# Gated linear unit of a hybrid decoder layer taken in halves by position, with a new written order of the work around it

## The chip, the cores and the metric

The kernel runs on one core of one Trainium2 chip. The metric is the device time of one execution in microseconds. The engines are named as in the profile: PE (TensorE matmuls), PEld (its weight loads), DVE (VectorE), ACT (ScalarE), POOL (GpSimd) and SP (SyncE, which issues the DMAs here).

## The reference

One decoder layer on 1024 positions with 1024 channels, in f32. The input projection z = x w_in is cut into S5 input, S5 gate gs, latents of attention, and an attention gate gm. What the change touches is the S5 head group:

```python
z = x @ w_in[i]
xs, gs, cq, ckv, kr, gm = jnp.split(z, IN_SPLIT_POINTS, axis=-1)
# s5_branch: diagonal complex state space over positions, then
y = jax.nn.gelu(y)
y = y * jax.nn.sigmoid(y @ w_glu.astype(f32) + b_glu.astype(f32))
...
ys = s5_branch(xs, ...) * jax.nn.silu(gs)
ym = mla_branch(cq, ckv, kr, cos, sin, ...) * jax.nn.silu(gm)
mix = jnp.concatenate([ys, ym], axis=-1) @ w_out[i]
u = DEEPNORM_ALPHA * x + mix
ple = jax.nn.sigmoid(u @ w_pg[i]) * (p[i] @ w_pp[i])
x = layer_norm(u + ple, ln_g[i], ln_b[i])
```

The attention has 4 heads, causal, with 1024 queries and keys.

## The kernel before, in words

Activations lie with channels on the 128 partitions and positions along the free axis. Every f32 operand of a matmul is split into a rounded high part and the rest (names ending in h and l: wh, wl; yTh, yTl; ysh, ysl): `split` makes the high part with a cast on ACT or DVE and the low part with a subtraction on DVE or POOL. A product is then three matmuls into the same PSUM tile (`mm3`). Matmuls move at most 512 columns, so most things come in two halves of 512, called hf 0 and 1.

The stages, in the order in which the PE goes through them: the products of p (pp), the layer norm and transposes of x (xt), the projections of the S5 input (xs, L743), then the list MAIN: eight half tiles of the attention gate (gm, L763), eight tiles of latents (lat, L787) and eight half tiles of the S5 gate (gs, L753). A projection half tile is 24 matmuls of 512 columns. Each needs its weight loaded (`w_load`, 512 KB from HBM) and split (`w_split`, tiles wh and wl); the latents need four weights split by `wt_split` (wth, wtl). Then comes attention over the 16 items of ATTEND (a head h and a block j of 256 queries): scores, softmax on DVE and ACT, transposes of the probabilities, product with the latent values, and uv_out, which multiplies by the gate gm and writes ymh and yml. Then the output projection (op) for eight channel tiles m and two halves, which reads ysh, ysl of the S5 group and ymh, yml of attention, and last the gate with p (g) and the final layer norm.

The S5 layer works on 8 interleaved phases: position 8n + j is held as phase j, index n, so that a scan has 128 steps. Its four blocks b each have `mats` (three pieces, DVE and PE), `in` (a load), `usplit`, `state` (tiles re, im, rt, hh, hu; the scans on DVE) and `out` (gelu, and a store to d_y). `glu_y(k)` (L1256) loads block k's y, laid out as phase j by index n, and splits it into yTh and yTl. `glu_gs(m)` (L1264) loads the S5 gate back from d_gs. `glu(m, hf)` (L1268) forms one of eight GLU half tiles: 12 matmuls of 512 columns, a sigmoid, a product with y, a product with the gate, and a split into ysh and ysl. A half here is four of the eight phases, so it covers all positions at a stride; the gate is stored in that layout as well (L753), and the split writes through `perm`, at a stride of 8 elements, into the order of positions that the output projection reads.

Other work hangs on the steps: the lists S5, LAT and GLU say at which step (a half tile or latent tile of MAIN, or an item of attention) a piece is written into the program. The order in which engines get instructions is not this written order. The class Plan records all operations with what they read and write, and `issue` (L304) places them one by one: always the operation that can start soonest by its own table of costs, and among those that can start at once the one with the lowest priority number. That number is the place in the written order plus a shift: SHIFT gives one per list (S5 -350, LAT -750, GLU -1250: these operations go ahead of that many written before them), AHEAD adds one per kind of piece (empty before), and in attention S5's shift is S5_LATE. Tiles come from pools with fixed numbers of buffers (40 of 4 KB per partition, 12 of 2 KB, 4 single and 2 double PSUM banks) and are given out in the written order, so this order decides also who gets a buffer first. For operations that may run on either of two engines (a split's high part on ACT or DVE, its low part on DVE or POOL) the planner chooses. All instructions are issued from L437, so the profile shows this one line and they are told apart by their tiles.

Of the kernel before, what the change touches and what calls it, by code (L numbers as in the profile page):

```python
# [25 lines left out]
F32 = mybir.dt.float32  # L26
F32R = mybir.dt.float32r
I32 = mybir.dt.int32
AF = mybir.ActivationFunctionType
# [5 lines left out]
P = 128  # L35
S = 1024
D = 1024
NK = D // P
H = 4
G = 32  # L40
CT = 8
NCH = S // CT
# [10 lines left out]
def _cw_parts(c, bits, n):  # L53
# [11 lines left out]
PI_LO = float(np.nextafter(np.float32(math.pi), np.float32(0)))  # L65

MAIN = [
    ("w_load", 10), ("gm", 0, 0), ("gm", 0, 1), ("w_split", 9), ("w_load", 11), ("gm", 1, 0), ("gm", 1, 1),
    ("w_split", 10), ("wt_load",), ("gm", 2, 0), ("gm", 2, 1), ("w_split", 11), ("gm", 3, 0), ("gm", 3, 1),
    ("wt_split", 0), ("wt_split", 1), ("wt_split", 2), ("wt_split", 3), ("lat", 0), ("lat", 1), ("lat", 2),  # L70
    ("lat", 3), ("w_load", 4), ("lat", 4), ("lat", 5), ("w_load", 5), ("lat", 6), ("lat", 7), ("w_split", 4),
    ("w_load", 6), ("gs", 0, 0), ("gs", 0, 1), ("w_split", 5), ("w_load", 7), ("gs", 1, 0), ("gs", 1, 1),
    ("w_split", 6), ("gs", 2, 0), ("gs", 2, 1), ("w_split", 7), ("gs", 3, 0), ("gs", 3, 1),
]


S5 = [
    (0, "in", 0), (0, "mats", 0), (0, "mats", 0), (0, "mats", 1), (0, "mats", 0), (0, "usplit", 0), (0, "state", 0),
    (2, "mats", 1), (5, "in", 1), (5, "mats", 1), (5, "usplit", 1), (5, "out", 0), (7, "mats", 2), (7, "state", 1),
    (7, "out", 1), (8, "mats", 2), (8, "mats", 2), (9, "phase", 1), (9, "in", 2), (13, "usplit", 2),  # L80
    (14, "state", 2), (14, "mats", 3), (16, "out", 2), (16, "in", 3), (18, "mats", 3), (23, "mats", 3),
    (25, "usplit", 3), (27, "state", 3), (30, "out", 3),
]
LAT = [
    (4, "lat_alloc"), (18, "lat_norm", 0), (19, "lat_transpose", 0), (19, "lat_norm", 1), (19, "lat_transpose", 1),
    (20, "fold"), (20, "q_rope", 0), (23, "q_rope_t", 0), (23, "q_rope", 1), (23, "mask"), (23, "q_nope", 0, 0),
    (24, "q_nope", 0, 1), (24, "q_rope_t", 1), (27, "q_nope", 1, 0), (27, "q_nope", 1, 1), (27, "q_nope", 2, 0),
    (28, "q_nope", 2, 1), (35, "q_nope", 3, 0), (35, "q_nope", 3, 1),
]
GLU = [  # L90
    (31, "glu_y", 0), (31, "glu_w"), (33, "glu_gs", 1), (35, "glu_y", 2), (35, "glu_gs", 2), (36, "glu_y", 1),
    (39, "glu_gs", 0), (39, "glu_gs", 3), (39, "glu_y", 3), (40, "glu", 0, 0), (40, "wo_load", 1),
    (41, "glu", 0, 1), (41, "wo_load", 0), (41, "glu", 1, 0), (42, "glu", 1, 1), (42, "glu", 2, 0),
    (42, "wo_split", 0), (42, "glu", 2, 1), (42, "glu", 3, 0), (42, "glu", 3, 1),
]
GATE = [(t, 0) for t in range(3)] + [(t, 1) for t in range(3)] + [(t, c) for t in range(3, 8) for c in range(2)]
ATTEND = [(h, j) for h in range(H) for j in (0, 3, 1, 2)]
S5_LATE = -400
AHEAD = {}
SHIFT = [(S5, -350), (LAT, -750), (GLU, -1250)]  # L100


class _Engine:
# [337 lines left out]
def trunk(ctx, tc, I, out):  # L441
# [10 lines left out]
    dr = ctx.enter_context(tc.tile_pool(name="dr", bufs=1, space=DRAM))  # L452
# [3 lines left out]
    def nm(s):  # L456
        cnt[0] += 1
        return f"{s}{cnt[0]}"

    def U(name, dt=F32, shape=(P, 1024)):  # L460
        return plan.own(up.tile(list(shape), dt, name=nm(name), tag="u"), "u", NU)

    def Hf(name, dt=F32, shape=(P, 512)):
        return plan.own(hp.tile(list(shape), dt, name=nm(name), tag="h"), "h", NHF)
# [10 lines left out]
    def PB(name, shape=(P, 512), dt=F32):  # L475
        return plan.own(psB.tile(list(shape), dt, name=nm(name), tag="B"), "B", 4)

    def f(ap):
        return ap.bitcast(F32)

    def mul(o, a, b, e=V):
        e.tensor_tensor(out=o, in0=a, in1=b, op=ALU.mult)
# [4 lines left out]
    def sub(o, a, b, e=V):  # L487
        e.tensor_tensor(out=o, in0=a, in1=b, op=ALU.subtract)
# [7 lines left out]
    def act(o, a, fn, scale=1.0, bias=None, accum=None):  # L496
        kw = {}
        if bias is not None:
            kw["bias"] = bias
        if accum is not None:  # L500
            kw["accum_out"] = accum
        A.activation(out=o, in_=a, func=fn, scale=scale, **kw)

    def cpy(e, o, a):
        plan.copy(e._name, o, a)

    def split(hi, lo, src, eh=AV, el=None):
        cpy(eh, hi, src)
        sub(lo, src, f(hi), el or (V if src.space == PSUM else VG))

    def mm(ps, a, b, st, sp_):
        T.matmul(ps, a, b, start=st, stop=sp_)

    def mm3(ps, ah, al, bh, bl, st, sp_):
        mm(ps, ah, bh, st, False)
        mm(ps, ah, bl, False, False)
        mm(ps, al, bh, False, sp_)
# [23 lines left out]
    def pexp(o, x, shape):  # L541
# [25 lines left out]
        out=ident, in_=ident, pattern=[[-1, P]], compare_op=ALU.is_equal, fill=0.0, base=0, channel_multiplier=1  # L567
# [16 lines left out]
    d_y = dr.tile([4, CT, P, NCH], F32, name="d_y")  # L584
    d_k = dr.tile([4, 15, 16, P], F32, name="d_k")
    d_gm = dr.tile([4, P, S], F32, name="d_gm")
    d_gs = dr.tile([4, P, CT, NCH], F32, name="d_gs")
    d_ut = dr.tile([8, P, D], F32, name="d_ut")


# [139 lines left out]
    def proj(m, hf):  # L730
        h, l = wq[m]
        ps = PB("z")
        s = slice(hf * 512, hf * 512 + 512)
        for k in range(NK):
            mm3(ps, h[:, k], l[:, k], xh[k][:, s], xl[k][:, s], k == 0, k == NK - 1)
        return ps

    def perm(ap):
        return ap.rearrange("p (n j) -> p j n", j=CT)
# [11 lines left out]
    gs = {}  # L751

    def gs_tile(m, hf):  # L753
        ps = proj(4 + m, hf)
        if hf == 0:
            gs[m] = U("gs", shape=(P, CT, NCH))
        act(gs[m][:, :, hf * 64 : hf * 64 + 64], perm(ps), AF.Silu)
        if hf == 1:
            SY.dma_start(out=d_gs[m], in_=gs[m])

# [482 lines left out]
    Y = {}  # L1243
    ysT = {}
# [17 lines left out]
        Y[k] = y, h, l  # L1262

    def glu_gs(m):  # L1264
        g = Y["gs", m] = U("gsr", shape=(P, CT, NCH))
        SY.dma_start(out=g, in_=d_gs[m])

    def glu(m, hf):  # L1268
        if hf == 0:
            ysT[m] = U("ysh", F32R), U("ysl", F32R)  # L1270
        ps = PB("glu")
        s = slice(hf * 512, hf * 512 + 512)
        for k in range(4):
            wh, wl = Y["w", k]
            ms = slice(m * P, m * P + P)
            mm3(ps, wh[:, ms], wl[:, ms], Y[k][1][:, s], Y[k][2][:, s], k == 0, k == 3)
        sg = Hf("sg")
        act(sg, ps, AF.Sigmoid, bias=Y["b"][:, m : m + 1])
        mul(sg, sg, Y[m][0][:, s])
        sg = sg.rearrange("p (j n) -> p j n", j=4)  # L1280
        j4 = slice(hf * 4, hf * 4 + 4)
        mul(sg, sg, Y["gs", m][:, j4])
        split(perm(ysT[m][0])[:, j4], perm(ysT[m][1])[:, j4], sg)


    uT = {}
# [182 lines left out]
    mats = [s5_mats(b) for b in range(4)]  # L1469
    for m in range(4):  # L1470
# [13 lines left out]
        "mats": lambda b: next(mats[b], None), "phase": s5_phase, "in": s5_in, "usplit": s5_usplit,  # L1484
        "state": s5_state, "out": s5_out, "lat_alloc": lat_alloc, "lat_norm": lat_norm,
        "lat_transpose": lat_transpose, "fold": fold, "q_rope": q_rope, "q_rope_t": q_rope_t,
        "q_nope": q_nope, "mask": mask_init, "glu_w": glu_w, "glu_y": glu_y, "glu_gs": glu_gs, "glu": glu,
        "wo_load": wo_load, "wo_split": wo_split,
    }

    main = {
        "w_load": w_load, "w_split": w_split, "wt_load": wt_load, "wt_split": wt_split,
        "gm": gm_tile, "lat": lat_tile, "gs": gs_tile,
    }
    steps = [0]

    def after(late=False):
        for stream, shift in SHIFT:
            for at, name, *args in stream:
                if at == steps[0]:  # L1500
                    plan.shift = (S5_LATE if stream is S5 and late else shift) + AHEAD.get(name, 0)
                    work[name](*args)
        plan.shift = 0
        steps[0] += 1

    for name, *args in MAIN:
        main[name](*args)
# [110 lines left out]
```

## Time and profile before

| | |
|---|---|
| median of 3 runs | 610.16 us (607.33 to 611.25) |
| the profiled execution | 605.49 us |
| its span, first to last instruction | 603.8 us |
| mean granted PE clock | 0.986 |
| HBM traffic | 50.47 MB read, 25.66 MB written |

How to read the profile: a stage's row gives, for a stretch of the span, the busy time of each engine with its number of instructions, the granted PE clock as a share of full speed, the busy share of the DMA engines and GB/s. A row of waits names who waited, for whom, total us, times, and the longest. A row of groups gives engine, operation, out<-in, shape and count, then busy time and mean ns of one, then the engine's idle time before them. A timeline row gives start and duration in us, and in brackets the idle time before it and what ended it. In the rows of one tile's instructions the durations are min/median/max in ns, with the first and last start.

### The profile page before, as it was taken

Reading aid. Unit: us, or ns where it says so; the run is one execution under the profiler, and the core shown is the slowest. Engines: PE = TensorE matmul, PEld = TensorE weight load, DVE = VectorE, ACT = ScalarE, POOL = GpSimd, SP = SyncE. Lnnn points to the kernel's source line nnn. Section 1 sums busy time; section 2 is a strip of 40 time slices with the busy share of each in tenths; the row PEclk is TensorE's granted clock in tenths of the full one; section 3 lists DMA queues with packets and bytes.
Section 4 is the critical chain, followed back from the end, with each engine's and each line's share of the span. In section 5 each row is a group of like instructions: output and inputs, shape, how many; then the busy total and the mean of one; then the engine's idle time right before and its main releaser. Section 6 shows DMA issues by size and latency. Waiting matters only on the chain.

```text
span 603.8 us, 8361 instructions
## 1 busy us (share of the span) xinstructions
PE 569.3 (94%) x3000; PEld 484.9 (80%) x3000; DVE 447.7 (74%) x958; ACT 287.2 (48%) x527; POOL 83.1 (14%) x104
## 2 busy tenths in 40 slices
PE   8999989699899999999799999996999999999994
PEld 6777878587698888889699999874888888888884
DVE  6999999999989774677979888686323225567666
ACT  6767245463643853357579667552222135233121
POOL 0100001200201133041432313103000001000000
PEclk9999999989999999999999999997999999999998
DMA  8898233620330511201024224425242426924301
GB/s 314 322 356 283 94 105 108 209 72 37 110 104 1 192 69 41 69 37 36 0 71 141 67 75 146 141 87 219 71 139 71 156 85 241 354 78 167 105 35 71
DMA packets 46233, 76.66 MB, mean 127 GB/s; under 512 B 4384, under 2 KB 27104, under 8 KB 46192
## 3 DMA queue, kind: packets, MB, share of 16 engines
q1 hardware_dynamic: 46192, 76.14, 36.6%
q8 instruction: 23, 0.38, 0.3%
q14 instruction: 18, 0.15, 0.1%
HBM read 50.47 MB, written 25.66 MB: 126 GB/s over the span
## 4 chain that ended last, share of the span: by engine, by line
PE 52%; DVE 8%; ACT 3%; DMA 1%; issue 1%; POOL 1%; DVEq 0%; ACTq 0%; POOLq 0%
PE g L437 14%; PE op L437 14%; PE s L437 6%; PE z L437 5%; PE o L437 3%; PE pt L437 2%; DVE sg L437 2%; PE qn L437 1%; DVE ysl L437 1%; PE ut L437 1%; DMA yT<-d_y 1%; ACT ysh L437 1%; PE qrp L437 1%; PE y L437 1%; DVE rt L437 1%
## 5 line engine op out<-in xcount | busy, mean ns | idle before, releaser
L437 PE MATMUL z<-xh,wl 128*128 128x512 f32 x192 | 75.6, 395 | 6.3 <-DVE wl L437 6.3
L437 PE MATMUL z<-xh,wh 128*128 128x512 f32 x192 | 75.7, 394 | 0.0
L437 PE MATMUL z<-xl,wh 128*128 128x512 f32 x192 | 75.6, 394 | 0.0
L437 PE MATMUL g<-wph,uh 128*128 128x512 f32 (+1 forms) x136 | 51.4, 378 | 0.0
L437 PE MATMUL g<-wph,ul 128*128 128x512 f32 (+1 forms) x136 | 51.2, 377 | 0.0
L437 PE MATMUL g<-wpl,uh 128*128 128x512 f32 (+1 forms) x136 | 51.2, 377 | 0.0
L437 DVE SCALAR_TENSOR_TENSOR xr<-xr,op 128x512 f32<-128x512 f32 x16 | 11.0, 687 | 51.9 <-PE op L437 51.9
L437 PEld LDWEIGHTS z<-xh,wl 128*128 128x128 f32 x192 | 36.2, 188 | 13.9 <-DVE wl L437 7.2
L437 PEld LDWEIGHTS z<-xh,wh 128*128 128x128 f32 x192 | 36.2, 189 | 7.0
L437 PEld LDWEIGHTS z<-xl,wh 128*128 128x128 f32 x192 | 36.1, 188 | 6.7
L437 PE MATMUL op<-ysh,woh 128*128 128x512 f32 x64 | 26.8, 419 | 4.4 <-DVE ysh L437 4.4
L437 PEld LDWEIGHTS g<-wpl,uh 128*128 128x128 f32 x136 | 25.6, 188 | 4.7
L437 PEld LDWEIGHTS g<-wph,uh 128*128 128x128 f32 x136 | 25.6, 188 | 4.7
L437 PEld LDWEIGHTS g<-wph,ul 128*128 128x128 f32 x136 | 25.6, 188 | 4.6
L437 ACT ACTIVATE p<-p,mx 128x128 f32<-128x128 f32 (+7 forms) x32 | 24.7, 772 | 9.2 <-DVE mx L437 9.2
L437 DVE CUSTOM_DVE_ANT_0 p<-s,mask 128x128 f32<-128x128 f32 (+7 forms) x32 | 24.1, 753 | 5.7 <-PE s L437 5.2
L437 PE MATMUL op<-ysl,woh 128*128 128x512 f32 x64 | 25.8, 402 | 1.1 <-POOL ysl L437 0.6
L437 ACT CAST uh<-xr 128x512 fp32r<-128x512 f32 x15 | 9.3, 621 | 36.1 <-DVE xr L437 32.8
L437 DVE TENSOR_TENSOR ptl<-pt,pth 128x512 fp32r<-128x512 f32 (+3 forms) x48 | 25.2, 551 | 1.5 <-ACT pth L437 1.0
L437 ACT ACTIVATE sgg<-g 128x512 f32<-128x512 f32 (+1 forms) x17 | 9.6, 564 | 33.5 <-PE g L437 33.5
L437 PE MATMUL op<-ysh,wol 128*128 128x512 f32 x64 | 25.5, 399 | 0.0
L437 PE MATMUL op<-ymh,woh 128*128 128x512 f32 x64 | 25.4, 397 | 0.0
(363 smaller groups left out, 1660.2 us busy)
## 6 DMA issues: line engine op xcount, KB each, us to landing
wr<-in_w_fm SPq DMA_DIRECT2D x12, 512.0 KB, 6.1
x<-in_x SPq DMA_DIRECT2D x8, 512.0 KB, 8.3
d_pp<-ppo SPq DMA_DIRECT2D x8, 512.0 KB, 4.8
d_xln<-xt SPq DMA_DIRECT2D x16, 256.0 KB, 6.2
wor<-in_w_out SPq DMA_DIRECT2D x8, 512.0 KB, 5.4
xr<-d_xln SPq DMA_DIRECT2D x8, 512.0 KB, 4.6
d_ut<-ut SPq DMA_DIRECT2D x16, 256.0 KB, 2.4
utok<-d_ut SPq DMA_DIRECT2D x16, 256.0 KB, 4.3
```

The lines of the kernel that those rows point to most:

```text
L437: getattr(self.real[ran[i]], method)(*ops[i]["args"], **kw)
```

## The change

It has two parts. First, a GLU half tile becomes half of the positions: `cols` picks from each of the eight phases the 64 indices of this half, so the matmul's moving operand is 8 runs of 64 columns; the sigmoid reads PSUM in the order of positions and writes sg contiguously; the gate gs is stored and loaded in the order of positions; `glu_yg(m)`, a new piece, multiplies the loaded gate by y for all 1024 positions before GLU, reading y with a stride; and what is left after the sigmoid is one product and a split, both contiguous. Second, the lists MAIN, S5, LAT, GLU and ATTEND, the shifts and AHEAD are given anew. Matmuls, loads and stores stay the same in number and size.

```diff
 MAIN = [
-    ("w_load", 10), ("gm", 0, 0), ("gm", 0, 1), ("w_split", 9), ("w_load", 11), ("gm", 1, 0), ("gm", 1, 1),
-    ("w_split", 10), ("wt_load",), ("gm", 2, 0), ("gm", 2, 1), ("w_split", 11), ("gm", 3, 0), ("gm", 3, 1),
-    ("wt_split", 0), ("wt_split", 1), ("wt_split", 2), ("wt_split", 3), ("lat", 0), ("lat", 1), ("lat", 2),
-    ("lat", 3), ("w_load", 4), ("lat", 4), ("lat", 5), ("w_load", 5), ("lat", 6), ("lat", 7), ("w_split", 4),
-    ("w_load", 6), ("gs", 0, 0), ("gs", 0, 1), ("w_split", 5), ("w_load", 7), ("gs", 1, 0), ("gs", 1, 1),
-    ("w_split", 6), ("gs", 2, 0), ("gs", 2, 1), ("w_split", 7), ("gs", 3, 0), ("gs", 3, 1),
+    ("w_load", 11), ("w_split", 11), ("gm", 0, 0), ("gm", 0, 1), ("w_load", 10), ("w_split", 10), ("w_split", 9),
+    ("gm", 1, 0), ("gm", 1, 1), ("wt_load",), ("gm", 2, 0), ("gm", 2, 1), ("gm", 3, 0), ("wt_split", 2),
+    ("w_load", 4), ("wt_split", 0), ("wt_split", 1), ("wt_split", 3), ("lat", 0), ("gm", 3, 1), ("lat", 1),
+    ("lat", 2), ("lat", 6), ("lat", 7), ("lat", 4), ("w_load", 5), ("lat", 3), ("lat", 5), ("w_load", 6),
+    ("w_split", 5), ("gs", 1, 0), ("w_split", 4), ("w_load", 7), ("w_split", 6), ("w_split", 7), ("gs", 1, 1),
+    ("gs", 0, 0), ("gs", 0, 1), ("gs", 2, 0), ("gs", 2, 1), ("gs", 3, 0), ("gs", 3, 1),
 ]
 S5 = [
-    (0, "in", 0), (0, "mats", 0), (0, "mats", 0), (0, "mats", 1), (0, "mats", 0), (0, "usplit", 0), (0, "state", 0),
-    (2, "mats", 1), (5, "in", 1), (5, "mats", 1), (5, "usplit", 1), (5, "out", 0), (7, "mats", 2), (7, "state", 1),
-    (7, "out", 1), (8, "mats", 2), (8, "mats", 2), (9, "phase", 1), (9, "in", 2), (13, "usplit", 2),
-    (14, "state", 2), (14, "mats", 3), (16, "out", 2), (16, "in", 3), (18, "mats", 3), (23, "mats", 3),
-    (25, "usplit", 3), (27, "state", 3), (30, "out", 3),
+    (0, "mats", 0), (0, "in", 0), (0, "mats", 1), (0, "mats", 0), (0, "mats", 0), (0, "usplit", 0), (0, "state", 0),
+    (3, "mats", 1), (4, "mats", 1), (4, "in", 1), (4, "usplit", 1), (6, "out", 0), (7, "mats", 2), (7, "state", 1),
+    (7, "in", 2), (8, "out", 1), (8, "mats", 2), (9, "mats", 2), (9, "usplit", 2), (11, "phase", 1), (12, "state", 2),
+    (12, "out", 2), (14, "mats", 3), (17, "in", 3), (17, "mats", 3), (20, "mats", 3), (24, "usplit", 3),
+    (26, "state", 3), (32, "out", 3),
 ]
 LAT = [
-    (4, "lat_alloc"), (18, "lat_norm", 0), (19, "lat_transpose", 0), (19, "lat_norm", 1), (19, "lat_transpose", 1),
-    (20, "fold"), (20, "q_rope", 0), (23, "q_rope_t", 0), (23, "q_rope", 1), (23, "mask"), (23, "q_nope", 0, 0),
-    (24, "q_nope", 0, 1), (24, "q_rope_t", 1), (27, "q_nope", 1, 0), (27, "q_nope", 1, 1), (27, "q_nope", 2, 0),
-    (28, "q_nope", 2, 1), (35, "q_nope", 3, 0), (35, "q_nope", 3, 1),
+    (11, "lat_alloc"), (17, "lat_norm", 1), (18, "lat_transpose", 1), (18, "lat_norm", 0), (18, "mask"),
+    (19, "lat_transpose", 0), (20, "fold"), (20, "q_rope", 0), (21, "q_rope", 1), (23, "q_rope_t", 0),
+    (23, "q_nope", 0, 0), (24, "q_nope", 0, 1), (24, "q_rope_t", 1), (27, "q_nope", 1, 0), (27, "q_nope", 2, 0),
+    (27, "q_nope", 1, 1), (28, "q_nope", 2, 1), (30, "q_nope", 3, 0), (30, "q_nope", 3, 1),
 ]
 GLU = [
-    (31, "glu_y", 0), (31, "glu_w"), (33, "glu_gs", 1), (35, "glu_y", 2), (35, "glu_gs", 2), (36, "glu_y", 1),
-    (39, "glu_gs", 0), (39, "glu_gs", 3), (39, "glu_y", 3), (40, "glu", 0, 0), (40, "wo_load", 1),
-    (41, "glu", 0, 1), (41, "wo_load", 0), (41, "glu", 1, 0), (42, "glu", 1, 1), (42, "glu", 2, 0),
-    (42, "wo_split", 0), (42, "glu", 2, 1), (42, "glu", 3, 0), (42, "glu", 3, 1),
+    (31, "glu_w"), (32, "glu_y", 2), (35, "glu_y", 1), (37, "glu_y", 0), (37, "glu_gs", 1), (37, "glu_yg", 1),
+    (39, "glu_y", 3), (39, "glu_gs", 2), (39, "glu_yg", 2), (39, "glu_gs", 3), (39, "glu_yg", 3), (39, "wo_load", 1),
+    (39, "glu", 1, 0), (40, "wo_load", 0), (40, "glu_gs", 0), (40, "glu_yg", 0), (40, "glu", 0, 0), (40, "glu", 0, 1),
+    (41, "glu", 2, 0), (42, "wo_split", 0), (42, "glu", 3, 0), (42, "glu", 2, 1), (42, "glu", 1, 1),
+    (42, "glu", 3, 1),
 ]
-ATTEND = [(h, j) for h in range(H) for j in (0, 3, 1, 2)]
-S5_LATE = -400
-AHEAD = {}
-SHIFT = [(S5, -350), (LAT, -750), (GLU, -1250)]
+ATTEND = [
+    (0, 0), (0, 3), (0, 1), (0, 2), (1, 0), (1, 3), (2, 0), (2, 1), (1, 1), (2, 2), (1, 2), (2, 3), (3, 0), (3, 2),
+    (3, 1), (3, 3),
+]
+S5_LATE = -20
+AHEAD = {"fold": 200, "glu": -930, "glu_gs": -110, "glu_w": -60, "glu_y": 300, "in": 400, "lat_alloc": -500, "lat_norm": -160, "lat_transpose": -1100, "mask": -400, "mats": -170, "out": 30, "phase": -300, "q_nope": 30, "q_rope": 500, "q_rope_t": 200, "state": -400, "usplit": 30, "wo_load": 30, "wo_split": -30}
+SHIFT = [(S5, -2560), (LAT, -760), (GLU, -2090)]
...
-    d_gs = dr.tile([4, P, CT, NCH], F32, name="d_gs")
+    d_gs = dr.tile([4, P, S], F32, name="d_gs")
...
         if hf == 0:
-            gs[m] = U("gs", shape=(P, CT, NCH))
-        act(gs[m][:, :, hf * 64 : hf * 64 + 64], perm(ps), AF.Silu)
+            gs[m] = U("gs")
+        act(gs[m][:, hf * 512 : hf * 512 + 512], ps, AF.Silu)
...
     def glu_gs(m):
-        g = Y["gs", m] = U("gsr", shape=(P, CT, NCH))
+        g = Y["gs", m] = U("gsr")
         SY.dma_start(out=g, in_=d_gs[m])
 
+    def glu_yg(m):
+        g = Y["gs", m].rearrange("p (n j) -> p n j", j=CT)
+        mul(g, g, Y[m][0].rearrange("p (j n) -> p n j", j=CT))
+
     def glu(m, hf):
...
-        s = slice(hf * 512, hf * 512 + 512)
+        cols = lambda x: x.rearrange("p (j n) -> p j n", j=CT)[:, :, hf * 64 : hf * 64 + 64]
         for k in range(4):
             wh, wl = Y["w", k]
             ms = slice(m * P, m * P + P)
-            mm3(ps, wh[:, ms], wl[:, ms], Y[k][1][:, s], Y[k][2][:, s], k == 0, k == 3)
+            mm3(ps, wh[:, ms], wl[:, ms], cols(Y[k][1]), cols(Y[k][2]), k == 0, k == 3)
+        s = slice(hf * 512, hf * 512 + 512)
         sg = Hf("sg")
-        act(sg, ps, AF.Sigmoid, bias=Y["b"][:, m : m + 1])
-        mul(sg, sg, Y[m][0][:, s])
-        sg = sg.rearrange("p (j n) -> p j n", j=4)
-        j4 = slice(hf * 4, hf * 4 + 4)
-        mul(sg, sg, Y["gs", m][:, j4])
-        split(perm(ysT[m][0])[:, j4], perm(ysT[m][1])[:, j4], sg)
+        act(sg.rearrange("p (n j) -> p n j", j=CT), ps.rearrange("p (j n) -> p n j", j=CT), AF.Sigmoid, bias=Y["b"][:, m : m + 1])
+        mul(sg, sg, Y["gs", m][:, s])
+        split(ysT[m][0][:, s], ysT[m][1][:, s], sg)
```

More of the change, by code (lines that the diff above doesn't have):

```diff
@@ L1486, in trunk @@
         "lat_transpose": lat_transpose, "fold": fold, "q_rope": q_rope, "q_rope_t": q_rope_t,
-        "q_nope": q_nope, "mask": mask_init, "glu_w": glu_w, "glu_y": glu_y, "glu_gs": glu_gs, "glu": glu,
+        "q_nope": q_nope, "mask": mask_init, "glu_w": glu_w, "glu_y": glu_y, "glu_gs": glu_gs,
+        "glu_yg": glu_yg, "glu": glu,
         "wo_load": wo_load, "wo_split": wo_split,
```

## The prediction

> **What bounds the kernel now.** I read the page first, then the busy time by stage, then what the PE waited for, then the timeline around the two longest PE waits.
>
> ```profile
> span 603.8 us, 8361 instructions
> PE 569.3 (94%) x3000; PEld 484.9 (80%) x3000; DVE 447.7 (74%) x958; ACT 287.2 (48%) x527; POOL 83.1 (14%) x104
> ```
>
> The PE is busy for 569.3 of 603.8 us. The change takes away no matmul (one form of them gets another access pattern), so it can only win where the PE does not stream. The sum is made against the profiled execution: 605.49 us, of which 603.8 are span and 1.7 lie around it. The median of the three runs shown, 610.16, stands 4.67 above it; I carry this offset over and forecast a median.
>
> The stages: 100 to 160 us holds the projections of the MLA gate and the first S5 blocks, 160 to 280 the latents and S5 gates, 280 to 380 attention, 380 to 404 mainly GLU, 404 to 420 the way into the output projection.
>
> ```profile
> core 0: us, PE busy (x) PEld busy (x) DVE busy (x) ACT busy (x) POOL busy (x), PEclk, DMA share, GB/s
> 100.00:122.00 22.00, 16.04 (x79) 12.74 (x78) 21.61 (x42) 8.90 (x24) 3.24 (x5) 0.93 0.53 183
> 122.00:140.00 18.00, 17.76 (x92) 15.60 (x91) 16.43 (x21) 12.79 (x16) 0.11 (x1) 0.89 0.21 71
> 140.00:160.00 20.00, 17.01 (x89) 13.56 (x88) 19.80 (x34) 6.47 (x12) 1.28 (x1) 1.00 0.18 67
> 160.00:280.00 120.00, 119.12 (x665) 105.08 (x663) 91.11 (x190) 64.73 (x143) 28.86 (x31) 1.00 0.21 72
> 280.00:300.00 20.00, 16.27 (x107) 14.06 (x105) 18.37 (x46) 10.38 (x20) 7.36 (x7) 1.00 0.04 16
> 300.00:380.00 80.00, 79.43 (x558) 73.79 (x559) 66.64 (x183) 60.16 (x127) 22.59 (x29) 1.00 0.34 107
> 380.00:404.00 24.00, 23.71 (x120) 20.09 (x119) 17.15 (x23) 12.71 (x16) 1.02 (x1) 1.00 0.24 86
> 404.00:420.00 16.00, 10.46 (x37) 7.43 (x36) 13.08 (x16) 5.79 (x8) 4.99 (x3) 0.79 0.59 229
> ```
>
> The losses stand in three places. From 100 to 160 the PE is idle for 5.96 + 0.24 + 2.99 = 9.2 us while the DVE is busy for 57.8 of 60: the DVE bounds that stretch. From 280 to 300 it is idle for 3.7, with the DVE at 18.4 of 20. From 404 to 420 it is idle for 5.5 and the granted clock is 0.79. In the 200 us of 160:280 and 300:380 it lost 1.5.
>
> ```profile
> PE z L437 <- DVE wl L437: 6.3, 2, 5.3
> PE op L437 <- DVE ysh L437: 4.4, 1, 4.4
> PE zl L437 <- DVE wtl L437: 2.0, 1, 2.0
> ```
>
> So the largest waits are for the low half of a projection weight (wl, written by w_split), for ysh, the GLU result that the output projection reads, and for wtl, the low half of a latent weight. Now the GLU wait from close by:
>
> ```profile
> 404.54 0.28 PE L437 MATMUL uv<-ol,wuv 128*128 128x256 f32 x1
> 404.66 0.28 PE L437 MATMUL uv<-oh,wuvl 128*128 128x256 f32 x1
> 404.78 0.40 PE L437 MATMUL op<-ysh,woh 128*128 128x512 f32 x1
> 405.01 0.40 PE L437 MATMUL op<-ysl,woh 128*128 128x512 f32 x1
> ...
> 413.03 0.62 DVE L437 CAST ysh<-sg 128x512 fp32r<-128x512 f32 x1
> 413.79 2.64 POOL L437 TENSOR_TENSOR ysl<-sg,ysh 128x512 fp32r<-128x512 f32 x1 [28.77 <-DVE ysh L437]
> 413.80 0.76 PE L437 MATMUL op<-ysh,woh 128*128 128x512 f32 x1 [4.40 <-DVE ysh L437]
> ```
>
> Successive matmuls start 0.12 us apart at 256 columns and 0.23 at 512, though each is shown as 0.28 or 0.40 long. The eighth and last sigmoid starts at 405.4 (the row of sg<-glu further down), but its ysh is made at 413.03 and its ysl ends at 416.43: eleven microseconds for an epilogue of four instructions, because seven earlier ones stand before it. Of the 37 matmuls in 404:420 about 33 have 512 columns and 4 have 256: at full rate 33 x 0.23 + 4 x 0.12 = 8.1 us. The stage took 16, so **7.9 us** are lost there, idle time and slow clock together.
>
> **The change part by part.**
>
> *GLU by position.* The rows of its epilogue before, and those of the same operations without a permuted write:
>
> ```profile
> L437 ACT ACTIVATE sg<-glu,b_glu x8: 656/678/688, 382.0 to 405.4; 128x512 f32<-128x512 f32 x8
> L437 DVE TENSOR_TENSOR sg<-sg,yT x8: 673/688/759, 383.7 to 410.5; 128x512 f32<-128x512 f32 x8
> L437 DVE TENSOR_TENSOR sg<-sg,gsr x8: 684/692/1117, 384.5 to 412.1; 128x512 f32<-128x512 f32 x8
> L437 DVE TENSOR_TENSOR ysl<-sg,ysh x7: 1074/1193/1256, 386.9 to 411.1; 128x512 fp32r<-128x512 f32 x7
> L437 ACT CAST ysh<-sg x6: 1132/1172/1191, 385.7 to 409.5; 128x512 fp32r<-128x512 f32 x6
> ```
>
> ```profile
> L437 DVE TENSOR_TENSOR ul<-xr,uh 128x512 fp32r<-128x512 f32 x16 | 11.1, 692 | 11.1 <-ACT uh L437 11.1
> ...
> L437 ACT CAST uh<-xr 128x512 fp32r<-128x512 f32 x15 | 9.3, 621 | 36.1 <-DVE xr L437 32.8 <-issue 3.3
> ...
> L437 DVE TENSOR_TENSOR tl<-tr,th 128x1024 fp32r<-128x1024 f32 x4 | 4.9, 1215 | 0.6 <-ACT th L437 0.6
> ```
>
> Before, one tile costs the DVE 0.69 + 0.69 + 1.19 = 2.57 us and the ACT 0.68 + 1.17 = 1.85, against 12 x 0.23 = 2.76 on the PE. Weight splits and attention share the DVE, so it falls behind. After, one product goes and the split writes contiguously, as for uh and ul: DVE 0.69 + 0.69 = 1.38, ACT 0.68 + 0.62 = 1.30. Eight tiles save the DVE 9.5 us and the ACT 4.4. The sigmoid now reads PSUM in another order, which no quoted row has: between nothing and what the permuted write cost the cast, 0.55 us (1172 less 621) x 8 = 4.4. The ACT is busy for 12.7 of 24 us in this stage, so even 4.4 is hidden, and I take 0; without that cover it would be 4.4.
>
> Added are four products of 1024 elements, formed beforehand, whose second operand is read with a stride. No row has just this. Bounds are 1.2 us (tl, 1024 elements in short runs) and 2.4 (twice ysl, a strided write). I take 1.8, so 7.2 us in all, between 4.8 and 9.6: the DVE's net is about -2, and none of it is left on the way to the output projection.
>
> The larger gain is in what is awaited. A half was four of the eight interleaved phases, spread over all positions, so every out_proj half needed all eight GLU tiles. Now out_proj's first half needs only the four tiles of positions 0 to 511. The last of these is fifth in the written order, and three further tiles (3 x 2.76 = 8.3 us of PE) cover its 0.68 + 0.69 + 0.62 + 0.69 = 2.7 us of epilogue. The eighth tile's epilogue is covered by 24 matmuls of out_proj's first half (5.5 us). What is late next is the last attention block, (3, 3), of head 3's last positions: the second halves alone read it. I let 0.6 us remain of the 7.9: **-7.3**. Ends: 0 (the wait moves) and -7.9.
>
> *The moving operand of the 96 GLU matmuls* becomes 8 runs of 64 columns. No matmul of this trace reads so. Bounds: nothing, or each break between runs costs what cutting a 512 in two costs (2 x 0.12 - 0.23 = 0.01), seven breaks 0.07, x 96 = **+6.7 us**, all on the PE. I take 0, as runs of 64 are nearer to whole rows than to single elements.
>
> The Trainium skill (Advanced Engine Details and Errata, section Memory Cachelines) speaks against that: it says that "Any non-contiguous AP significantly slows down matmuls", of PSUM, while in SBUF accesses within a 16-byte line are at full speed. By the first sentence the sum would lose up to all of the GLU gain, by the second nothing, as the output here stays contiguous; no run so far shows either.
>
> *The gate loads* (gsr) now feed a DVE product right behind them.
>
> ```profile
> gsr<-d_gs SPq DMA_DIRECT2D x4, 512.0 KB, 4.8
> ```
>
> Size and count are unchanged, as for the store. The planner's own constants give 0.46 + 0.9 + 1.46 + 0.9 = 3.7 us; a landing takes 4.8. If all four are awaited, the DVE stands 4 x 1.1 = 4.4 us, with attention's mask and ptl queued behind it, and the PE behind those. From 300 to 404 the DVE has 20.2 us free (83.8 of 104 busy), which hides it; without that cover it costs 4.4. I take 0.
>
> *Order of projections.* The wait of 2.0 us for wtl came as the four wt_splits stood behind S5's chain. Now gm(3, 1), 24 x 0.23 = 5.5 us, is written between the first two latent tiles, and wt_split 2 before the other three: -2.0 (ends -2.0, 0). The wait of 5.3 for wl looks so:
>
> ```profile
> 116.85 2.76 DVE L437 TENSOR_TENSOR hh<-rt,rt 64x508 f32<-64x508 f32 x4
> 119.64 1.23 DVE L437 TENSOR_TENSOR wl<-wr,wh 128x1024 fp32r<-128x1024 f32 x1
> ...
> 137.61 0.42 DVE L437 TENSOR_TENSOR re<-w,wt 64x256 f32<-64x256 f32 x1
> ...
> 153.89 1.29 DVE L437 TENSOR_TENSOR hu<-hh,hu 128x512 fp32r<-128x512 f32 x2
> ```
>
> This wl stood behind the state step (scans, rt, hh) of S5's block 0. The change writes the splits of weights 11 and 10 ahead of gm(0, 0), which helps, but puts 9, the one that gm(1) reads, third, and raises S5's lead over everything else from 350 operations to 2560, which hurts: whatever S5 has ready goes first. With the slower clock behind it, the place is worth 5.3 + 18 x (1 - 0.89) = 7.3 us either way. I take 0.
>
> *Order of S5 and attention.* State 3 comes one step earlier (26, not 27); in attention its lead is 20 + 400 = 420 where it was 400. Its 18.4 of 20 busy DVE microseconds are the same work at the same place: 0, ends -3.7 (the idle time of 280:300) and +3.7.
>
> *Sum:* -7.3 - 2.0 = -9.3. The profiled 605.49 becomes 596.2, the median 610.16 becomes **600.9 us**.
>
> **The rivals.**
>
> 1. *The wl wait goes too:* the splits of 11 and 10 come ahead of S5's state 0, and 9's finds a gap in its chain. For: their early place, and a chain that leaves gaps between dependent instructions. Against: S5's larger lead. 600.9 - 7.3 = 593.6.
>
> 2. *The gain is eaten:* the 8 runs cost the PE 6.7 us, or the gate loads 4.4 with a repeat of the wtl wait, 2.0, or gm(1) repeats the 5.3 wait. For: nothing in the trace shows a split moving operand; DVE bounds 100 to 160. Against: what is written late there is small. About 600.9 + 6.7 = 607.6.
>
> 3. *Slower: S5's block 2 gets in front of the weight splits.* Its usplit, state and out are written at steps 9 to 12 instead of 13 to 16, some 10 us sooner, and with a lead of 2560 they pass every split. For block 1 the stretch from re to hu on the DVE ran from 137.6 to 155.1, 17.5 us. If a split that the PE's next tile needs stands behind such a stretch, the PE has one half tile (5.5 us) for cover and loses 12, and the clock falls as it did after 120.9, another 2: +14. It decides as soon as state 2 is ready before the splits of 9, 10 or wt are done. For: the DVE was busy for 57.8 of 60 there. Against: block 2 waits for its own load and matrices first. 600.9 + 14 + 2.0 (the wtl wait stays) = 616.9.
>
> **How the numbers follow.** The forecast gets 0.55, rival 1 0.16, rival 2 0.17 (0.06 for the 8 runs, which alone would make 607.6, and 0.11 for the others), rival 3 0.12. A measurement of this kernel tells about 1%, 6.1 us, from no change: faster means under 604.1, slower over 616.3. The forecast's own range is 595 to 606, so 0.50 of its 0.55 is faster and 0.05 is the same. Faster: 0.50 + 0.16 = 0.66; same: 0.05 + 0.17 = 0.22; slower: 0.12. The range reaches down to 589 (forecast less 7.3 and less 3.7 is 589.9) and up to 611, past rival 2 with half of the 6.7 more; rival 3 and a little else are outside.
>
> **What would show it.** Right: the PE waits for ysh and ysl are under 1 us in sum, the granted clock stays at 1.00 where GLU meets the output projection, no ysl runs on POOL there, ysh takes about 620 ns and ysl 690, GLU matmuls still start 0.23 apart, and the wait for wtl is gone. Wrong: op waits for ymh, wol or a DMA instead; GLU matmuls start 0.30 apart (the 8 runs); the idle time of the PE from 100 to 160 is over 15 us (rival 3) or under 3 (rival 1); a DVE wait for gsr of more than 1 us. A time under 589 or over 611 would say that the order of the earlier stages, which I took as worth 2 us, decided the result.

## The result and the profile after

| kernel | median of its runs, us | before beside it, us | ratio, 95% interval |
|---|---|---|---|
| changed | 594.74 (592.97 to 595.81, 4 runs) | 610.08 | 0.9752 (0.9712 to 0.9792) |

The change makes the kernel 2.5% faster, 15.3 us by the medians. The forecast was 600.9 within 589 to 611, so the direction and the range held. But 594.74 lies just outside the 595 to 606 that the prediction called the forecast's own, and near rival 1's 593.6; the gain was 15.3 and not 9.3, and both terms of its sum were off, the one too large and the other too small. That the total came so near is in part luck. The profiled execution after took 592.97 us, 591.3 of them span.

The busy time by stage of the changed kernel, in the same columns as for before:

```profile
100.00:122.00 22.00, 21.39 (x105) 17.17 (x104) 21.65 (x39) 9.40 (x24) 5.58 (x7) 1.00 0.43 152
122.00:140.00 18.00, 18.00 (x104) 15.86 (x102) 16.25 (x25) 13.09 (x17) 3.43 (x2) 1.00 0.47 159
140.00:160.00 20.00, 19.56 (x105) 17.00 (x104) 19.90 (x31) 4.94 (x8) 0.11 (x1) 1.00 0.15 53
160.00:280.00 120.00, 117.20 (x657) 100.12 (x655) 97.57 (x202) 66.60 (x154) 29.29 (x33) 1.00 0.21 70
280.00:300.00 20.00, 19.39 (x121) 16.95 (x121) 19.68 (x47) 12.56 (x28) 8.74 (x8) 1.00 0.00 1
300.00:360.00 60.00, 58.90 (x426) 55.27 (x425) 50.76 (x141) 44.21 (x95) 16.28 (x20) 1.00 0.24 80
360.00:380.00 20.00, 17.46 (x99) 14.93 (x98) 17.32 (x33) 13.48 (x26) 2.07 (x3) 0.91 0.67 237
380.00:404.00 24.00, 24.00 (x127) 20.64 (x126) 18.38 (x28) 11.53 (x19) 2.41 (x3) 1.00 0.33 118
404.00:420.00 16.00, 16.00 (x76) 13.28 (x75) 6.39 (x8) 4.24 (x7) 0.60 (x1) 1.00 0.52 185
```

Since the changed kernel runs ahead of the one before, the same microseconds hold partly other work; the places below are where the difference is large. From 100 to 160 us the PE is idle for 1.05 us and not 9.2, with the DVE as full as before (57.8 of 60): the same DVE, another order on it. From 404 to 420 the PE is full and the clock is at 1.00. From 280 to 300 the PE is idle for 0.6 and not 3.7. And 160 to 280 became worse (2.8 idle, before 0.9), as did 360 to 380 (2.5 idle at a clock of 0.91, before 0.5 at 1.00).

The longest waits of the PE after (who, for whom, total us, times, longest):

```profile
PE pt L441 <- ACT sg L441: 2.2, 1, 2.2
PE wt L441 <- ACT bbh L441: 2.1, 1, 2.1
PE xt L441 <- DVE xt L441: 1.6, 3, 0.7
PE warm L441 <- DVE z L441: 1.5, 1, 1.5
PE pt L441 <- DVE ol L441: 1.4, 2, 1.1
PE z L441 <- DVE krh L441: 1.2, 1, 1.2
```

No wait for ysh or ysl is left among them, the 5.3 us wait for wl is gone (one of 1.1 us is left), and the wait for wtl fell from 2.0 to 0.4. At the top stands a new one: attention's transposes (pt) wait for sg, the sigmoid that frees a PSUM tile, at the start of GLU. The GLU epilogue after:

```profile
L441 ACT ACTIVATE sg<-glu,b_glu x8: 682/689/691, 372.3 to 400.8; 128x512 f32<-128x512 f32 x8
L441 DVE TENSOR_TENSOR sg<-sg,gsr x8: 684/690/695, 374.3 to 401.8; 128x512 f32<-128x512 f32 x8
L441 DVE TENSOR_TENSOR ysl<-sg,ysh x8: 685/691/693, 375.7 to 403.3; 128x512 fp32r<-128x512 f32 x8
L441 ACT CAST ysh<-sg x7: 621/622/629, 375.0 to 402.5; 128x512 fp32r<-128x512 f32 x7
```

The last sigmoid starts at 400.8 and the last ysl at 403.3: 3.2 us from the start of the one to the end of the other, where it was 11. The sigmoid reads PSUM in the new order in 689 ns (678 before).

### The profile page after: what moved, and what is told of

The parts are those of the page before. It is cut to its first block, busy times and chain, and to the rows that moved or that the text cites. A ratio compares the mean times of both kernels' runs of the same rounds, so it can differ in the third digit from the quotient of the medians.

```text
span 591.3 us, 8335 instructions
## 1 busy us (share of the span) xinstructions
PE 567.1 (96%) x3000; PEld 482.3 (82%) x3000; DVE 446.8 (76%) x952; ACT 281.6 (48%) x533; POOL 83.8 (14%) x100
## 4 chain that ended last, share of the span: by engine, by line
PE 57%; DVE 4%; issue 1%; ACT 1%; DVEq 0%
PE op L441 15%; PE g L441 15%; PE s L441 6%; PE o L441 4%; PE z L441 4%; PE glu L441 3%; PE pt L441 2%; PE qn L441 2%; PE ut L441 1%; PE uv L441 1%; PE qrp L441 1%; DVE gsr L441 1%; PE y L441 1%; DVE p L441 1%; DVE hh L441 0%
## 5 line engine op out<-in xcount | busy, mean ns | idle before, releaser
L441 ACT COPY ut<-ut 128x512 f32<-128x512 f32 x16 | 9.4, 588 | 35.3 <-PE ut L441 35.2
L441 PE MATMUL pt<-ident,p 128*128 128x128 f32 x144 | 21.5, 285 | 3.8 <-ACT sg L441 2.2
L441 POOL TENSOR_TENSOR rstd<-ve,half 128x1 f32<-128x1 f32 (+1 forms) x10 | 7.1, 714 | 126.2 <-DVE ve L441 107.6
```

The lines of the kernel that those rows point to most:

```text
L441: getattr(self.real[ran[i]], method)(*ops[i]["args"], **kw)
```

## The experiments

Each ran beside the kernel of before on the same chip; the ratios are to that.

| run | median, us | ratio, 95% interval |
|---|---|---|
| glu_only | 604.13 | 0.9937 (0.9912 to 0.9962) |
| order_only | 594.45 | 0.9786 (0.9754 to 0.9819) |
| before_new_main | 613.03 | 1.0085 (1.0059 to 1.0110) |
| after_old_main | 616.43 | 1.0127 (1.0095 to 1.0159) |
| after_yg_pool | 596.18 | 0.9807 (0.9774 to 0.9840) |
| glu_halves_only | 602.60 | 0.9907 (0.9884 to 0.9930) |
| after_s5_350 | 591.79 | 0.9730 (0.9701 to 0.9759) |
| after_old_head | 599.49 | 0.9861 (0.9840 to 0.9883) |
| s5_350_no_yg | 586.54 | 0.9653 (0.9635 to 0.9671) |
| before_new_head | 611.41 | 1.0061 (1.0045 to 1.0078) |
| glu_yg_only | 603.91 | 0.9932 (0.9911 to 0.9952) |
| after_old_attend | 593.59 | 0.9774 (0.9744 to 0.9804) |

### The two parts alone: glu_only and order_only

The new GLU form in the old lists, with the new pieces added to the old GLU list. The edit of that list, against the kernel of before (the new form itself is as in the change):

```diff
 GLU = [
-    (31, "glu_y", 0), (31, "glu_w"), (33, "glu_gs", 1), (35, "glu_y", 2), (35, "glu_gs", 2), (36, "glu_y", 1),
-    (39, "glu_gs", 0), (39, "glu_gs", 3), (39, "glu_y", 3), (40, "glu", 0, 0), (40, "wo_load", 1),
+    (31, "glu_y", 0), (31, "glu_w"), (33, "glu_gs", 1), (35, "glu_y", 2), (35, "glu_gs", 2), (35, "glu_yg", 2),
+    (36, "glu_y", 1), (36, "glu_yg", 1), (39, "glu_gs", 0), (39, "glu_yg", 0), (39, "glu_gs", 3), (39, "glu_y", 3),
+    (39, "glu_yg", 3), (40, "glu", 0, 0), (40, "wo_load", 1),
...
```

> The new GLU form (halves by position, product of gate and y beforehand) in the old written order; the new pieces stand right behind the later of their two loads. Theory A, the two parts add and GLU is worth what its stage shows between the two traces (from 360 to 420 us the PE lost 11.7 us before and 5.9 after): about 604, with the waits of the output projection for ysh and ysl under 1 us and the 5.3 us wait for wl still there. Rival, the form pays only with its new order of tiles: 608 to 610. Rival, GLU is the whole gain: 595.

The other way round, the new lists on the old GLU form, so without the four new pieces. The edit of the list, against the changed kernel (the old form itself is as before the change):

```diff
-    (31, "glu_w"), (32, "glu_y", 2), (35, "glu_y", 1), (37, "glu_y", 0), (37, "glu_gs", 1), (37, "glu_yg", 1),
-    (39, "glu_y", 3), (39, "glu_gs", 2), (39, "glu_yg", 2), (39, "glu_gs", 3), (39, "glu_yg", 3), (39, "wo_load", 1),
-    (39, "glu", 1, 0), (40, "wo_load", 0), (40, "glu_gs", 0), (40, "glu_yg", 0), (40, "glu", 0, 0), (40, "glu", 0, 1),
+    (31, "glu_w"), (32, "glu_y", 2), (35, "glu_y", 1), (37, "glu_y", 0), (37, "glu_gs", 1),
+    (39, "glu_y", 3), (39, "glu_gs", 2), (39, "glu_gs", 3), (39, "wo_load", 1),
+    (39, "glu", 1, 0), (40, "wo_load", 0), (40, "glu_gs", 0), (40, "glu", 0, 0), (40, "glu", 0, 1),
...
```

> The new written order, shifts and leads with the old GLU form (the four new pieces left out of the list). Theory A: about 600, as the projections and S5 (80 to 160 us) lost 16.4 us of PE before and 4.7 after, and the wait for ysh at the output projection stays at 4 us or so. Rival, the order was made for the new form and loses without it: 606 or more. Rival, the order is the whole gain: 595.

GLU alone is worth 0.6%, some 4 us; the order alone is worth 2.1%, some 13 us, and is not told apart from the whole change (0.9786 against 0.9752, with intervals that overlap). For GLU theory A's time came (604 expected, 604.13 measured), and its signs with it: no wait for ysh or ysl among those of the PE, and the 5.3 us wait for wl still there. For the order the time of the rival "the order is the whole gain" came (595). Whether the two parts add is not decided: 0.9937 x 0.9786 = 0.9724 is not told apart from the whole change's 0.9752 either. The profile of glu_only says why its gain is small, in its stages from 360 on:

```profile
360.00:384.00 24.00, 21.61 (x154) 19.54 (x153) 23.26 (x58) 15.50 (x35) 6.54 (x8) 1.00 0.50 174
384.00:404.00 20.00, 18.55 (x85) 15.59 (x85) 11.01 (x19) 7.30 (x12) 0.73 (x1) 0.91 0.16 54
404.00:420.00 16.00, 16.00 (x73) 13.30 (x72) 13.28 (x18) 7.55 (x11) 1.89 (x2) 1.00 0.61 231
```

The stall from 404 to 420 is gone as forecast, but from 360 to 404 the PE now sits idle for 2.4 + 1.4 us with the DVE at 23.3 of 24: the wait moved ahead, into the end of attention. The rows of waits name it:

```profile
PE glu L438 <- DVE ptl L438: 2.3, 1, 2.3
PE pt L438 <- DVE ol L438: 1.0, 1, 1.0
```

Where each profiled execution stood, by the start of the last matmul of the projections (z), of GLU and of the output projection (op), in us:

| run | z | GLU | op |
|---|---|---|---|
| before | 267.3 | 404.1 | 506.8 |
| changed | 258.5 | 400.4 | 494.3 |
| glu_only | 268.7 | 411.3 | 505.2 |
| order_only | 257.5 | 398.6 | 495.6 |
| s5_350_no_yg (below) | 255.7 | 393.3 | 487.1 |

The changed kernel is 8.8 us ahead of before at the end of the projections, 3.7 at the end of GLU and 12.5 at the end of the output projection. In glu_only the way from the last GLU matmul to the last of the output projection takes 93.9 us where it took 102.7, which is 8.8 gained, but 5.8 are lost between the projections and the end of GLU. order_only, with the old form, gains 5.7 us on that way too, so the new order takes a part of the same wait; its PE still waits 2.0 us for ysh and ysl.

### Which half of the GLU form: glu_halves_only, glu_yg_only, after_yg_pool

Halves by position with y multiplied after the sigmoid, in the old order. What the piece `glu` has more than that of the changed kernel (the four glu_yg entries are not in the list):

```diff
+        v = sg.rearrange("p (n j) -> p n j", j=CT)
+        mul(v, v, Y[m][0].rearrange("p (j n) -> p n j", j=CT)[:, hf * 64 : hf * 64 + 64])
         mul(sg, sg, Y["gs", m][:, s])
```

> The old written order, GLU halves by position but without the product of gate and y beforehand: y is multiplied per half after the sigmoid, read with a stride. Theory H, what the output projection waits for (four tiles and not eight) is what takes the 8 us wait away: 600 to 603, better than both together in the old order (604), as no long product stands in the way of attention. Rival, the shorter epilogue of the DVE is what does it: 606 to 608.

The old halves with the product beforehand in the phase layout, in the old order (against the kernel of before; the four entries in the list are those of glu_only):

```diff
+    def glu_yg(m):
+        g = Y["gs", m]
+        mul(g, g, Y[m][0].rearrange("p (j n) -> p j n", j=CT))
...
-        mul(sg, sg, Y[m][0][:, s])
```

> The old order and the old halves by phase, but the product of gate and y formed beforehand in the phase layout (no stride, about 1.2 us each), one product less per half. Theory H, the halves decide and the shorter epilogue does little: 607 to 609, with a wait of 3 us or more for ysh at the output projection. Rival, the DVE work is what counts: 603 to 605.

The halves alone give 0.9% and the product alone 0.7%; neither is told apart from both together (0.6%). So neither theory of the pair wins: in the first run theory H's time came (600 to 603), in the second its rival's (603 to 605). Each takes away a part of the wait for ysh and ysl (2.3 us of it are left with the halves alone, 2.5 with the product alone), and together, in glu_only, none of it is left. That they still give no more goes with the 2.3 us that the PE there waits for ptl, behind a product on the DVE; with the product alone this wait is 1.5.

The products of gate and y on POOL, in the changed kernel:

```diff
-        mul(g, g, Y[m][0].rearrange("p (j n) -> p n j", j=CT))
+        mul(g, g, Y[m][0].rearrange("p (j n) -> p n j", j=CT), Gp)
```

> The changed kernel with the four products of gate and y on POOL in place of the DVE. Theory Y, those products (1.99 us each on the DVE, two back to back) hold up ptl and ol of the last attention items and cost the PE the 5 us or so that it still loses from 360 to 380 us: about 591, with the PE's loss there down to 2. Rival, POOL takes 3 to 5 us for each and GLU's own product waits for it: 594 to 597.

The rival's time came: 596.18. A product takes 2.97 us on POOL against 1.99 on the DVE, and the PE then waits for yTl (2.3), ol (2.0) and yTh (0.9). That these products cost something had to be shown in another way, below (s5_350_no_yg).

### Where the order's gain comes from: after_old_head, before_new_head, the two MAIN lists, after_s5_350, after_old_attend

The loads and splits of weights 9 to 11 are put back where they were, and nothing else of the new lists:

```diff
-    ("w_load", 11), ("w_split", 11), ("gm", 0, 0), ("gm", 0, 1), ("w_load", 10), ("w_split", 10), ("w_split", 9),
-    ("gm", 1, 0), ("gm", 1, 1), ("wt_load",), ("gm", 2, 0), ("gm", 2, 1), ("gm", 3, 0), ...
+    ("w_load", 10), ("gm", 0, 0), ("gm", 0, 1), ("w_split", 9), ("w_load", 11), ("gm", 1, 0), ("gm", 1, 1),
+    ("w_split", 10), ("wt_load",), ("gm", 2, 0), ("gm", 2, 1), ("w_split", 11), ("gm", 3, 0), ...
```

> The changed kernel with the loads and splits of weights 9 to 11 written where they were before, the rest of the new list MAIN kept. Theory M, their early place lets the DVE make three wl ahead of block 0's scans: 600 or more, with a wait of some 5 us for wl. Rival, something else in the new lists does it: 594 to 596.

Theory M's early place is needed for a part of the gain: 599.49 (600 or more expected), and the two ratios (0.9861 and 0.9752) have intervals that do not touch. The difference is 1.1% or 6.6 us, and at the last projection matmul (265.0 against 258.5) it is all there; most of it arises from 80 to 160. First the row of the changed kernel, then that of after_old_head:

```profile
80.00:160.00 80.00, 76.86 (x394) 65.08 (x394) 77.39 (x122) 38.40 (x70) 13.84 (x12) 0.98 0.34 112
```

```profile
80.00:160.00 80.00, 72.91 (x368) 62.23 (x367) 76.68 (x129) 33.19 (x62) 12.80 (x13) 0.96 0.34 113
```

The same DVE time, 4 us less PE time and 26 matmuls fewer. But only 2.9 us of that are waits for wl (1.1 in the changed kernel); 2.8 more are for tl, a matrix of S5 (0.7). The same edit made the other way round, in the kernel of before:

> The kernel of before with the loads and splits of weights 9 to 11 written as early as in the new list, nothing else changed. Theory M, their place alone takes the wait for wl away: 602 to 604. Rival, it works only with the rest of the new lists: 608 or more, with a stall elsewhere.

The rival holds (608 or more): 611.41, 0.6% slower than before. The written place did not bring all three wl ahead of block 0's scans. Two came early (97.7 and 103.2), the third at 120.9:

```profile
L437 DVE TENSOR_TENSOR wl<-wr,wh x3: 1217/1217/1226, 97.6 to 120.9; 128x1024 fp32r<-128x1024 f32 x3
```

The wait for wl fell from 6.3 to 3.1 us, and another is now the longest:

```profile
PE zl L437 <- DVE wtl L437: 7.2, 1, 7.2
PE op L437 <- DVE ysh L437: 4.4, 1, 4.4
PE z L437 <- DVE wl L437: 3.1, 2, 2.0
```

The list MAIN as a whole was also exchanged, in both directions (`MAIN` of one kernel put for that of the other, nothing else):

> The kernel of before with the list MAIN alone taken from the new one. Theory M, the early written place of the weight splits of 10 and 11 takes away the wait for wl: about 601, the DVE makes three wl before S5's block 0 starts its scans. Rival S, it is S5's lists and the larger lead that make the stretch work: 608 to 611, with the wait of some 5 us for wl still there.

> The changed kernel with the list MAIN of before. Theory M: about 604, a wait of some 5 us for wl comes back and GLU's stage stays as after. Rival S: about 595 to 597.

The first is 0.9% slower than before, the second 1.3%; no theory had this. In the first the wl come as in before_new_head (98.1, 103.7 and 121.4, with 3.1 us of waits for them), the wait for wtl is not among the longest, and another has come, of the PE for hu, the S5 state that `out` multiplies:

```profile
PE y L437 <- DVE hu L437: 7.4, 1, 7.4
PE op L437 <- DVE ysh L437: 4.4, 1, 4.4
```

In the second the PE waits 8.2 us for uk, in `fold`, and 5.0 for wl. The S5 and LAT lists count steps of MAIN, so a new MAIN under old lists also shifts what hangs on the steps; these two runs show that the lists fit each other, not what either is worth.

S5's lead alone, in the changed kernel:

```diff
-SHIFT = [(S5, -2560), (LAT, -760), (GLU, -2090)]
+SHIFT = [(S5, -350), (LAT, -760), (GLU, -2090)]
```

> The changed kernel with S5's lead put back from 2560 to 350 operations. Theory L, the lead makes the stretch from 80 to 160 us work: 600 or more, with the wait for wl or for S5's chain back. Rival, it is where the weight splits are written, and the lead hardly decides: 594 to 596.

The rival holds: 591.79, if anything less than its 594 to 596 and than the changed kernel (0.9730 and 0.9752, not told apart). All three wl come as early as in the changed kernel (99.4 to 104.7). The large lead neither makes the gain nor costs much. Last, ATTEND of before in the changed kernel:

> The changed kernel with the order of attention items of before. If the new order of items is what cut the PE's loss from 280 to 300 us (6.0 to 2.3): 598 or more, with that loss back at 5 or 6 us. If it was S5's lists: 594 to 596, loss from 280 to 300 at 2 to 3.

593.59, and the stage from 280 to 300 is as good as with the new order of items:

```profile
280.00:300.00 20.00, 19.54 (x124) 17.42 (x123) 19.68 (x48) 11.93 (x28) 7.56 (x7) 1.00 0.00 1
```

So the order of the attention items decides nothing here, and nor does S5's lead (19.54 us busy in after_s5_350 too). What is left for this stage is MAIN, the lists S5, LAT and GLU, AHEAD and S5_LATE; none of them was tried by itself there.

### A version that beats both: s5_350_no_yg

The new lists with S5's lead at 350, halves by position, and no product beforehand (the edits of after_s5_350 and glu_halves_only, with the four glu_yg entries left out):

> The new order with S5's lead at 350, GLU halves by position, and no product of gate and y beforehand (y multiplied per half after the sigmoid). Theory Y, the products beforehand cost the PE most of the 5.4 us lost from 360 to 380: 587 to 589. Rival, the strided product per half (1.09 us) puts that loss at the output projection again: 591 to 594.

586.54 us, 0.9653 (0.9635 to 0.9671): 3.5% faster than before, and clear of after_s5_350 (0.9701 to 0.9759), from which it differs only in multiplying by y after the sigmoid and not beforehand. So with S5's lead at 350 the product beforehand, which the change adds, costs 0.8% (4.7 us) against a product per half. Theory Y had 587 to 589. Its stages where GLU begins, to be read against the rows 360:380 to 404:420 of the changed kernel:

```profile
360.00:380.00 20.00, 19.79 (x122) 17.34 (x121) 13.69 (x24) 12.30 (x21) 1.82 (x2) 1.00 0.55 193
380.00:404.00 24.00, 23.36 (x112) 19.42 (x111) 22.32 (x29) 13.29 (x20) 3.49 (x2) 1.00 0.51 198
404.00:420.00 16.00, 16.00 (x80) 13.29 (x79) 5.60 (x8) 4.44 (x7) 0.00 (x0) 1.00 0.29 87
```

The PE is idle for 0.85 us in these 60, and the changed kernel for 2.5 at a lower clock.

## Why the prediction was right or wrong

**The GLU wait (forecast -7.3, measured about -4 by glu_only).** The mechanism held, and at its own place it gave 8.8 us: with halves by position and the product beforehand the output projection no longer waits, the wait for ysh and ysl went from 5.5 us to under 1, the clock stayed at 1.00 from 404 to 420, and ysl no longer runs on POOL. The step that failed is "none of it is left on the way to the output projection", said of the products beforehand. They are not on that way, but on the way of the attention items that end at the same time. The DVE of the changed kernel at that point:

```profile
368.80 1.23 DVE L441 TENSOR_TENSOR yTl<-yT,yTh 128x1024 fp32r<-128x1024 f32 x1
369.94 3.78 DVE L441 TENSOR_TENSOR gsr<-gsr,yT 128x1024 f32<-128x1024 f32 x2
373.63 0.42 DVE L441 TENSOR_TENSOR ol<-o,oh 128x256 fp32r<-128x256 f32 x1
```

Two products run back to back for 3.78 us, with attention's ol behind them, while the PE stands:

```profile
370.41 0.40 PE L441 MATMUL glu<-yTh,wgl 128*128 128x512 f32 x1
371.01 1.28 ACT L441 ACT_TABLE_LOAD   x1
372.31 0.69 ACT L441 ACTIVATE sg<-glu,b_glu 128x512 f32<-128x512 f32 x1
373.05 0.80 PE L441 MATMUL pt<-ident,p 128*128 128x128 f32 x3 [2.24 <-ACT sg L441]
374.11 1.97 PE L441 MATMUL pt<-ident,p 128*128 128x128 f32 x8 [0.26 <-DVE ol L441]
```

Two things hold the PE here, one behind the other. The 2.24 us end with the first sigmoid, and 1.28 us of them are an ACT_TABLE_LOAD on the ACT right before it, for which the prediction had no term; the kernel of before has one of 1.28 us before its first sigmoid too, at 379.9, and its PE waits for no sg. The next transposes wait for ol, behind the products, which would have held them until 374.11 without the table load as well.

The price, 1.8 within 1.2 to 2.4, was right (1.99 measured); the place was not. The prediction set four products against what the shorter epilogue saves the DVE, a net of -2 us, and did not ask where in the order they run. s5_350_no_yg shows that the loss goes when the products go: there the PE waits neither for sg nor, at that place, for ol, and the table load starts only behind the casts of attention. How much of the 4.7 us is the DVE time of the products and how much the other place of the table load was not separated.

**The order (forecast -2.0, measured about -13 by order_only, which has a part of the GLU wait in it).** The step that failed is "the place is worth 5.3 + 18 x (1 - 0.89) = 7.3 us either way. I take 0." The wait for wl went, as rival 1 had it: its time (593.6) is nearer to the result than the forecast, and its sign, under 3 us of idle PE from 100 to 160, came (1.05). The prediction counts "the wait for wl is gone" among the signs of being right, though its sum left that wait in; it is a sign of rival 1. Its mechanism is in the trace of the changed kernel:

```profile
99.68 1.23 DVE L441 TENSOR_TENSOR wl<-wr,wh 128x1024 fp32r<-128x1024 f32 x1
100.81 0.84 DVE L441 TENSOR_TENSOR re<-w,wt 64x256 f32<-64x256 f32 x2
...
102.03 1.49 DVE L441 TENSOR_TENSOR wl<-wr,wh 128x1024 fp32r<-128x1024 f32 x1
103.55 0.87 DVE L441 TENSOR_TENSOR im<-w,wt 64x256 f32<-64x256 f32 x2
...
104.99 1.21 DVE L441 TENSOR_TENSOR wl<-wr,wh 128x1024 fp32r<-128x1024 f32 x1
...
108.00 1.47 DVE L441 TENSOR_TENSOR rt<-im,es 128x512 f32<-128x512 f32 x1
```

All three wl are made between 99.7 and 106.2, in the gaps of block 0's chain and ahead of its rt and scans; before, they came at 97.7, 119.6 and 130.0. What rival 1 did not see is that the written place alone does not bring this about: in before_new_head one wl still stands behind the scans, and the PE then waits for wtl (7.2 us); with the whole new MAIN in the old lists it waits for hu (7.4). That these later waits come from the same shortage of DVE time fits the DVE's 19.6 of 20 us from 140 to 160 in before_new_head, but was not tried. That the splits' place is needed is shown (after_old_head, 6.6 us), that it suffices is disproved; the same holds for MAIN as a whole. Which entries of the S5, LAT and GLU lists and of AHEAD do the rest stays open. S5's large lead is not needed (after_s5_350).

**The rest of the order.** The wait for wtl went as forecast (2.0 to 0.4). The idle time from 280 to 300 fell by 3.1, which I had at 0 within 3.7, though not by the order of attention items. 160 to 280 gave back 1.9, which had no term.

**The offset.** A part of the miss is no mechanism at all. The profiled execution was to take 596.2 and took 592.97, 3.2 us less; the median was to lie 4.67 above it, as before the change, and lay 1.77 above, another 2.9. The runs of before beside the experiments have medians from 608.06 to 608.29, so the 610.16 that the sum started from was on the high side.

**Terms taken as nothing.** The 8 runs of 64 columns cost nothing: GLU matmuls after start 0.23 apart, as shown here, so rival 2's 6.7 us did not come, and this run agrees with what the Trainium skill (Advanced Engine Details and Errata, section Memory Cachelines) says of accesses within a line of SBUF. Its sentence on access patterns that are not contiguous stands there under PSUM and was not tried, as the matmuls' output in PSUM stayed contiguous.

```profile
378.36 0.39 PE L441 MATMUL glu<-yTh,wgh 128*128 128x512 f32 x1
378.58 0.39 PE L441 MATMUL glu<-yTl,wgh 128*128 128x512 f32 x1
378.81 0.39 PE L441 MATMUL glu<-yTh,wgl 128*128 128x512 f32 x1
```

The gate loads cost the DVE one wait of 1.5 us, before 379.5, more than the 1 us that I had set as the mark for wrong. The PE lost nothing by it: it is busy throughout from 378 to 404. The sigmoid's new reading order added 11 ns to each of the eight (689 against 678); the prediction had bounded it by 550.

**Rival 3 (slower)** did not come: block 2 did not pass the splits, and after_s5_350 shows that the larger lead on which it rested hardly decides.

## What to carry to other kernels

Work that is moved off a critical chain on a shared engine is not free because the stage has slack on average: look at what stands right behind it on that engine at the moment when it runs. Where one engine is full for a long stretch, an order that takes away the longest wait by itself may only pass the shortage on to the next consumer, so judge a written order by the idle time of the whole stretch. And the two parts of a change are best timed apart: here the order by itself is not told apart from the whole change, and the other part held a step that cost 0.8%.

## What the runs showed of the hardware

A gap of about 2 us in the PE's work was in some executions followed by a halved granted clock, and in others a longer gap was not. In the changed kernel the PE waited 2.08 us before 82.3, and the clock in windows of 2 us then reads 0.77 and 0.50:

```profile
80.00:82.00 2.00, 0.21 (x1) 0.00 (x0) 2.00 (x3) 0.81 (x1) 0.00 (x0) 1.00 0.82 226
82.00:84.00 2.00, 1.71 (x9) 1.52 (x10) 2.00 (x4) 1.30 (x5) 0.00 (x0) 0.77 0.00 0
84.00:86.00 2.00, 2.00 (x6) 1.55 (x5) 2.00 (x3) 1.13 (x2) 0.00 (x0) 0.50 0.00 0
```

In after_s5_350 the wait at the same place was 2.58 us, and the clock stayed at 1.00:

```profile
82.43 0.90 PE L441 MATMUL wt<-ic,bbh 128*128 128x160 f32 x6 [2.58 <-ACT bbh L441]
82.00:84.00 2.00, 1.57 (x10) 1.43 (x11) 2.00 (x4) 1.30 (x5) 0.00 (x0) 1.00 0.00 0
84.00:86.00 2.00, 2.00 (x11) 1.62 (x10) 2.00 (x3) 1.15 (x3) 0.00 (x0) 1.00 0.00 0
```

In the kernel of before, the 2.0 us wait for wtl at 152 left it at 1.00, and the 2.24 us wait before 373.05 in the changed kernel brought 0.50 from 374 to 376. So the length of the gap alone does not decide here; what else does, no run shows. A stall that a change makes shorter, but not shorter than about 2 us, may still bring the slow clock behind it. The strided product also has its price now: 1.99 us for 1024 elements on the DVE when one operand is read at a stride of 128 elements, 1.24 when nothing is strided (glu_yg_only), 2.97 on POOL with the stride (after_yg_pool).
